# One transformer-like layer on one core: the products of a weight tile regrouped by width, and the tiles of the high weights moved by 192 bytes

## The chip, the core and the metric

The kernel runs on one core of a Trainium2 chip. The metric is the device time of one execution in microseconds. All weights lie in device memory in float32 and are streamed once per execution (277.83 MB read, by the page); everything else stays on the core.

## The reference, cut to what matters

One layer of a streaming encoder for 256 tokens of width 2048, with a memory of 256 more tokens:

```
u = rms_norm(h); proj = u @ w_in                       # 2048 -> 4944 columns
h = h + concat(gated_deltanet(...), mla_attention(...)) @ w_out
h = h + cross_attention(rms_norm(h), rms_norm(mem))    # xa_wq, xa_wk, xa_wv, xa_wo, all 2048 x 2048
u = causal_dwconv(rms_norm(h) @ w_up) + b              # 2048 -> 11264
h = h + (silu(gate) * up) @ w_down                     # 5632 -> 2048
return rms_norm(h)
```

Nearly all of the arithmetic is in the dense products with the seven weight matrices. All values are float32, and the result must be close to a float32 one.

## The kernel before, in words

**Three products for one.** Every float32 operand of a dense product is split into a high and a low part, both in the type that TensorE takes in one pass (float32r). The result is wh·xh + wh·xl + wl·xh. A tile of tokens holds xh in its columns 0 to 255 and xl in 256 to 511. So one step over 128 rows of the contraction, `kstep`, is two products: one of 512 columns with the high weights (wh on xh and xl at once, its halves are added after the sum), and one of 256 columns with the low weights (wl on xh). In this text they are H and L, and H and L of the same step are a pair. `kstep3` does the same in three products of 256 columns that add up in one place (wh on xh, wh on xl, wl on xh); the MLA part, the query projection, the cross-attention and the last block of the output use it. The value projection is written out by hand: the tokens of the memory are the weights there, and 512 columns of wh, wl and wh again are streamed over them (L981, L982, L983).

**Weight tiles.** `load_w` (L106) brings 128 x 1024 weights, eight steps, to a tile `raw` by a transfer on SyncE's queue. `split_w` makes wh by a rounding copy on ScalarE (L102) and wl by a subtraction on VectorE (L103). The three live in four buffers each of one pool. In the start, tiles come in halves (`piece`, L209).

**Order.** TensorE's order is the order of the code (a manual schedule, L189). The orders of the other engines are made by a scheduler from its own estimates. `kstep` alternates: H L, then L H, then H L, so that products of equal width follow each other in twos. In the DeltaNet and MLA parts the dense products serve as filler: a generator, `drawn` (L279), yields after each pair, and `fill(n)` and `until(n)` draw so many pairs between the small products, for instance 45 of them (`F_SOLVE`) while VectorE solves a small triangular system (tiles sol, prd, then tt).

**Places.** In the built program the tiles of tokens (u, om, od, mh, xq, xo, fx, ga, gb) begin at multiples of 256 bytes in each partition. So do kh, qh, pTx and vh, the operands of the cross-attention's small products. raw, wh and wl begin 64 bytes past such a multiple; a step within a weight tile is 512 bytes, so every 128 x 128 block of weights has the place of its tile.

Of the kernel before, what the change touches and what calls it, by code (L numbers as in the profile page):

```python
# [9 lines left out]
F32 = mybir.dt.float32  # L10
F32R = mybir.dt.float32r
# [6 lines left out]
F_BEFORE_MLA, F_BEFORE_DN1 = 8, 20  # L18
F_MLA, F_LEVEL, F_PRE, F_SOLVE = (6, 2, 4, 9), (3, 4, 5), (21, 6), 45
F_SCAN, F_NORM, F_SQ = 5, 28, 42  # L20

P = 128
T = 256
D = 2048
KC = D // P
DFF = 5632
NF = DFF // P
# [43 lines left out]
def trunk(ctx, tc, a):  # L71
    nc = tc.nc
    V, S, PE = nc.vector, nc.scalar, nc.tensor

    const = ctx.enter_context(tc.tile_pool(name="const", bufs=1))
    wpool = ctx.enter_context(tc.tile_pool(name="wpool", bufs=4))
# [5 lines left out]
    def psg():  # L82
        return pg.tile([P, 512], F32, name="psg", tag="psg")
# [12 lines left out]
    def split_w(raw, n, pieces=1):  # L96
        wh = wpool.tile([P, 1024], F32R, name="wh", tag="wh")
        wl = wpool.tile([P, 1024], F32R, name="wl", tag="wl")
        m = n // pieces
        for i in range(pieces):  # L100
            c = slice(i * m, (i + 1) * m)
            S.copy(wh[:, c], raw[:, c])  # L102
            V.tensor_sub(wl[:, c], raw[:, c], wh[:, c].bitcast(F32))  # L103
        return wh, wl

    def load_w(src, n=1024, pieces=1):  # L106
        raw = wpool.tile([P, 1024], F32, name="raw", tag="raw")
        nc.sync.dma_start(raw[:, 0:n], src)
        return split_w(raw, n, pieces)

    turn_ = [False]

    def kstep(ps, wh, wl, xh2, first, last):
        rev = turn_[0] and not first
        turn_[0] = not rev
        for lo in ((True, False) if rev else (False, True)):
            if lo:
                PE.matmul(ps[:, 0:256], wl, xh2[:, 0:256], start=False, stop=last, skip_group_check=True)  # L120
            else:
                PE.matmul(ps[:, 0:512], wh, xh2, start=first, stop=last, skip_group_check=True)  # L122

    def kstep3(ps, wh, wl, xh2, first, last):
        PE.matmul(ps[:, 0:T], wh, xh2[:, 0:T], start=first, stop=False)  # L125
        PE.matmul(ps[:, 0:T], wh, xh2[:, T:2 * T], start=False, stop=False)  # L126
        PE.matmul(ps[:, 0:T], wl, xh2[:, 0:T], start=False, stop=last)  # L127

    def gemm_block(w, nb, x, step=kstep):
        ps = psg()  # L130
        for hf in range(2):
            wh, wl = load_w(w[2 * nb + hf])
            for j in range(8):
                k = 8 * hf + j
                step(ps, wh[:, j * P:(j + 1) * P], wl[:, j * P:(j + 1) * P], x(k), k == 0, k == KC - 1)
        return ps
# [51 lines left out]
    u = hl_tile("u")  # L188
    ctx.enter_context(tc.manual_schedule(engines={mybir.EngineType.PE}))  # L189
    with ExitStack() as ph:  # L190
# [10 lines left out]
        first3 = []  # L201
        with tc.tile_pool(name="xpool", bufs=1) as xpl:
            xt = xpl.tile([P, KC, T], F32, name="xt")
            nc.sync.dma_start(sm[:, 0:KC], a["sm"][:, 0:KC])

            first3 += [psg(), psg(), psa("a")]
            w3 = {}

            def piece(nb, q):  # L209
                hf, c = q // 2, slice(q % 2 * 512, q % 2 * 512 + 512)  # L210
                if (nb, hf) not in w3:
                    w3[nb, hf] = [wpool.tile([P, 1024], t, name=nm, tag=nm)
                                  for nm, t in (("raw", F32), ("wh", F32R), ("wl", F32R))]
                raw, wh, wl = w3[nb, hf]
                nc.sync.dma_start(raw[:, c], a["w_in"][2 * nb + hf][:, c])
                S.copy(wh[:, c], raw[:, c])  # L216
                V.tensor_sub(wl[:, c], raw[:, c], wh[:, c].bitcast(F32))

            for q in range(4):
                for k in range(4 * q, 4 * q + 4, 2):  # L220
                    nc.sync.dma_start(xt[:, k:k + 2], a["x"][:, k:k + 2, :])
                    for i in (k, k + 1):
                        split_gain(u(i), xt[:, i], sm[:, C_MIX + i:C_MIX + i + 1])
                    if k % 4 == 0:
                        piece(0, q)
                for nb in range(3):
                    if nb:
                        piece(nb, q)
                    wh, wl = w3[nb, q // 2][1:]
                    for k in range(4 * q, 4 * q + 4):  # L230
                        j = k % 8
                        kstep(first3[nb], wh[:, j * P:(j + 1) * P], wl[:, j * P:(j + 1) * P], u(k), k == 0,
                              k == KC - 1)
            lead = load_w(a["w_in"][6], pieces=2)
            nc.sync.dma_start(cg, a["cg"])

            sqs = []
            for q in range(4):
                sqs.append(p1.tile([P, 4, T], F32, name="xsq", tag="qkv2", bufs=2))
                S.activation(sqs[q], xt[:, 4 * q:4 * q + 4], AF.Square)  # L240
                if q:
                    V.tensor_add(sqs[0], sqs[0], sqs[q])
            accs = [sqs[0][:, i] for i in range(4)]
            nc.sync.dma_start(sm[:, KC:NSM], a["sm"][:, KC:NSM])
            nc.sync.dma_start(co, a["co"][:, 0:NCO])
# [33 lines left out]
        def drawn():  # L279
            ready = {0: lead}  # L280
            ps = None
            i = 0
            while i < len(queue):
                for n in range(i, min(i + 1 + ahead[0], len(queue))):
                    if n not in ready:
                        ready[n] = load_w(queue[n][0], pieces=2)
                _, x, begin, first, last, done = queue[i]
                if begin:
                    begin()
                wh, wl = ready.pop(i)  # L290
                if first:
                    ps = psg()
                for j in range(8):
                    kstep(ps, wh[:, j * P:(j + 1) * P], wl[:, j * P:(j + 1) * P], x(j),
                          first and j == 0, last and j == 7)
                    if last and j == 7:
                        done(ps)
                    pos[0] += 1
                    for at_, f in [t for t in later if t[0] <= pos[0]]:
                        later.remove((at_, f))  # L300
                        f()
                    yield
                i += 1
# [77 lines left out]
        with ExitStack() as ms:  # L381
# [42 lines left out]
            ps = psa()  # L424
# [72 lines left out]
            ps = psa()  # L497
# [5 lines left out]
            ps = psa()  # L503
# [91 lines left out]
            for i in range(2):  # L595
                kn = mp.tile([P, 4, T], F32, name="kn", tag="kn")
                wh, wl = w_mla(i)
                for n in range(4):
                    ps = psg()
# [8 lines left out]
                wh, wl = w_mla(2 + i)  # L608
                for t in range(2):
                    ps = psg()  # L610
# [252 lines left out]
        od = hl_half("od")  # L863
# [72 lines left out]
    with ExitStack() as ph:  # L936
# [4 lines left out]
        for n in range(KC):  # L941
            wh, wl = load_w(a["w_out"][2 * n + 1])
            ps = psg()
            for j in range(8):
                kstep(ps, wh[:, j * P:(j + 1) * P], wl[:, j * P:(j + 1) * P], od[:, j], j == 0, j == 7)
            add_res(ps, n)
            if n < 8:
                mem_prep(8 + n)
# [10 lines left out]
        for n in range(KC):  # L959
            ps = gemm_block(a["xa_wk"], n, mh)  # L960
# [81 lines left out]

        def wo_half(ps, n, hf):
            wh, wl = load_w(a["xa_wo"][2 * n + hf])
            for j in range(8):
                k = 8 * hf + j
                kstep(ps, wh[:, j * P:(j + 1) * P], wl[:, j * P:(j + 1) * P], xo(k), k == 0, k == KC - 1)

        qhs, khs = {}, {}
        XS = float(512 ** -0.5)  # L1050
# [10 lines left out]
        xo = hl_tile("xo", x2pool)  # L1061
# [18 lines left out]
        for n in range(KC):  # L1080
            if n < 3:
                ps = pw[n]
            else:
                ps = psg()
# [10 lines left out]
    with ExitStack() as ph:  # L1095
# [3 lines left out]
        gk = lambda k: ga(k) if k < KC else gb[:, k - KC]  # L1099
# [35 lines left out]
        for n in range(KC):  # L1135
            ps = psg()
            for c in range(6):
                nk = 8 if c < 5 else 4
                o = n * NF * P + c * 1024
                wh, wl = load_w(a["w_down"][n, :, c * 1024:c * 1024 + nk * P], nk * P)  # L1140
                for j in range(nk):
                    k = 8 * c + j
                    (kstep if n < KC - 1 else kstep3)(ps, wh[:, j * P:(j + 1) * P], wl[:, j * P:(j + 1) * P],
                                                      gk(k), k == 0, k == NF - 1)
            if n < KC - 1:
                add_res(ps, n)
                accum_sq(oacc, hT[:, n], n == 0)
            else:
                V.tensor_add(hT[:, n], hT[:, n], ps[:, 0:T])
                lsq = small.tile([P, T], F32, name="lsq", tag="sq")  # L1150
                S.activation(lsq, hT[:, n], AF.Square)
            nc.gpsimd.tensor_scalar(hT[:, n], hT[:, n], sm[:, C_FIN + n:C_FIN + n + 1], None, ALU.mult)
# [119 lines left out]
```

## Time and profile before

| | us |
|---|---|
| median of 3 runs | 1577.72 (1575.12 to 1577.83) |
| the profiled execution | 1574.15 |
| its span, first to last instruction | 1572.3 |
| TensorE busy | 1542.3 (98%) |
| VectorE busy | 1117.3 (71%) |
| ScalarE busy | 888.5 (57%) |

The profile lists each engine's busy time and groups of equal instructions. A name such as psg<-fx,wh is output, streamed operand, weights. PE is TensorE; PEld is its weight loading, which overlaps the products. Matmuls overlap each other too: a product's listed length is longer than the distance at which products follow. So TensorE's share of 98% says that it hardly ever waits, and not how fast it works.

### The profile page before, as it was taken

How to read it: one execution, taken by the hardware profiler on the slowest of the kernel's cores; microseconds unless marked ns; L12 is line 12 of the kernel's file. 1: busy time of each engine (PE TensorE's matmuls, PEld its weight loads, DVE VectorE, ACT ScalarE, POOL GpSimd, SP SyncE). 2: the span in 40 equal slices, each digit the busy share in tenths (PEclk: the TensorE clock that was granted, in tenths of full speed). 3: DMA queues.
4: the chain of work that ended last, by engine and by line, in shares of the span. 5: the costliest groups of instructions: out<-in, count | busy, mean ns of one | idle time of the engine just before them, and what ended most of it. 6: DMA issues, size and time to landing. Idle time of an engine off the chain costs nothing.

```text
span 1572.3 us, 24569 instructions
## 1 busy us (share of the span) xinstructions
PE 1542.3 (98%) x9394; PEld 1357.5 (86%) x9394; DVE 1117.3 (71%) x1806; ACT 888.5 (57%) x1461; POOL 140.5 (9%) x145
## 2 busy tenths in 40 slices
PE   8999999999999999999999999999999999999996
PEld 7887887888888889999888888888888888888886
DVE  7887688697975555666777888888888886445453
ACT  7868666847664444454556666656665555434442
POOL 0232021002310000000110000000000000111112
PEclk9999999999999999999999999999999999999998
DMA  8564434354665555544555555555555556666663
GB/s 280 175 212 142 147 122 134 121 201 136 214 195 192 189 187 191 177 142 148 174 188 187 189 190 193 192 189 188 187 190 191 192 190 179 191 194 182 195 188 105
DMA packets 81494, 282.22 MB, mean 179 GB/s; under 512 B 9473, under 2 KB 9873, under 8 KB 81377
## 3 DMA queue, kind: packets, MB, share of 16 engines
q1 hardware_dynamic: 80064, 277.86, 54.7%
q0 software_dynamic: 1312, 2.80, 0.5%
q8 instruction: 73, 1.20, 0.3%
q14 instruction: 45, 0.36, 0.1%
HBM read 277.83 MB, written 2.11 MB: 178 GB/s over the span
## 4 chain that ended last, share of the span: by engine, by line
PE 88%; DVE 5%; ACT 4%; issue 1%; DMA 1%; POOL 0%; DVEq 0%; SPq 0%; ACTq 0%; POOLq 0%
PE psg L122 46%; PE psg L120 23%; PE psg L125 3%; PE psg L127 3%; PE psg L126 3%; DVE wl L103 2%; PE psg L983 2%; PE psg L982 2%; PE psg L981 2%; ACT wh L102 1%; DVE qkv L340 1%; PE psa L643 1%; PE psb L643 0%; PE psa L562 0%; DMA mt<-in_mem_dram 0%
## 5 line engine op out<-in xcount | busy, mean ns | idle before, releaser
L103 DVE TENSOR_TENSOR wl<-raw,wh 128x1024 fp32r<-128x1024 f32 (+1 forms) x602 | 641.0, 1071 | 278.5 <-ACT wh L102 271.3
L102 ACT CAST wh<-raw 128x1024 fp32r<-128x1024 f32 (+1 forms) x602 | 544.0, 915 | 393.7 <-PE psg L122 240.2
L122 PE MATMUL psg<-fx,wh 128*128 128x512 f32 x1408 | 439.8, 393 | 0.0
L120 PEld LDWEIGHTS psg<-fx,wl 128*128 128x128 f32 x1408 | 264.7, 188 | 59.8
L120 PE MATMUL psg<-fx,wl 128*128 128x256 f32 x1408 | 277.6, 279 | 0.0
L122 PEld LDWEIGHTS psg<-fx,wh 128*128 128x128 f32 x1408 | 212.2, 188 | 0.0
L122 PE MATMUL psg<-u,wh 128*128 128x512 f32 x608 | 200.6, 401 | 7.2 <-DVE u L149 7.2
L120 PEld LDWEIGHTS psg<-u,wl 128*128 128x128 f32 x608 | 115.3, 190 | 28.3 <-DVE wl L103 2.4
L140 ACT COPY half<-psg 128x256 f32<-128x256 f32 x142 | 52.6, 370 | 153.9 <-PE psg L122 153.7
L122 PE MATMUL psg<-gb,wh 128*128 128x512 f32 x420 | 133.4, 393 | 0.0
L120 PE MATMUL psg<-u,wl 128*128 128x256 f32 x608 | 130.3, 287 | 1.9 <-DVE wl L103 1.9
L122 PEld LDWEIGHTS psg<-u,wh 128*128 128x128 f32 x608 | 96.2, 190 | 9.5 <-ACT wh L216 7.2
L120 PEld LDWEIGHTS psg<-gb,wl 128*128 128x128 f32 x420 | 79.0, 188 | 17.9
L1112 DVE SCALAR_TENSOR_TENSOR y<-ub,sm,y 128x256 f32<-128x256 f32 x176 | 84.8, 482 | 3.5 <-ACT y L1110 0.3
L120 PE MATMUL psg<-gb,wl 128*128 128x256 f32 x420 | 82.8, 278 | 0.0
L122 PE MATMUL psg<-mh,wh 128*128 128x512 f32 x256 | 80.5, 394 | 0.0
L122 PE MATMUL psg<-xo,wh 128*128 128x512 f32 x256 | 80.4, 393 | 0.0
L141 DVE TENSOR_TENSOR ub<-psg,half 128x256 f32<-128x256 f32 x88 | 37.4, 425 | 59.7 <-ACT half L140 59.7
L122 PE MATMUL psg<-ga,wh 128*128 128x512 f32 x240 | 77.3, 393 | 0.0
L125 PE MATMUL psg<-xq,wh 128*128 128x256 f32 x256 | 71.2, 278 | 0.0
L126 PE MATMUL psg<-xq,wh 128*128 128x256 f32 x256 | 70.9, 277 | 0.0
L127 PE MATMUL psg<-xq,wl 128*128 128x256 f32 x256 | 70.9, 277 | 0.0
(411 smaller groups left out, 2430.1 us busy)
## 6 DMA issues: line engine op xcount, KB each, us to landing
raw<-in_w_up_dram SPq DMA_DIRECT2D x176, 512.0 KB, 3.5
raw<-in_w_down_dram SPq DMA_DIRECT2D x80, 512.0 KB, 4.3
raw<-in_w_in_dram SPq DMA_DIRECT2D x72, 512.0 KB, 3.9
raw<-in_w_out_dram SPq DMA_DIRECT2D x32, 512.0 KB, 3.6
raw<-in_xa_wk_dram SPq DMA_DIRECT2D x32, 512.0 KB, 3.5
raw<-in_xa_wv_dram SPq DMA_DIRECT2D x32, 512.0 KB, 3.4
raw<-in_xa_wq_dram SPq DMA_DIRECT2D x32, 512.0 KB, 3.5
raw<-in_xa_wo_dram SPq DMA_DIRECT2D x32, 512.0 KB, 3.4
```

What stands on the lines that cost most here:

```text
L102: S.copy(wh[:, c], raw[:, c])
L103: V.tensor_sub(wl[:, c], raw[:, c], wh[:, c].bitcast(F32))
L120: PE.matmul(ps[:, 0:256], wl, xh2[:, 0:256], start=False, stop=last, skip_group_check=True)
L122: PE.matmul(ps[:, 0:512], wh, xh2, start=first, stop=last, skip_group_check=True)
L125: PE.matmul(ps[:, 0:T], wh, xh2[:, 0:T], start=first, stop=False)
L126: PE.matmul(ps[:, 0:T], wh, xh2[:, T:2 * T], start=False, stop=False)
L127: PE.matmul(ps[:, 0:T], wl, xh2[:, 0:T], start=False, stop=last)
L140: S.copy(t, ps[:, T:2 * T])
L141: V.tensor_add(out, ps[:, 0:T], t)
L981: PE.matmul(pss[t], xh, wh[:, wk], start=(k == 0), stop=False)
L982: PE.matmul(pss[t], xh, wl[:, wk], start=False, stop=False)
L1112: V.scalar_tensor_tensor(y, b[:, j:j + T], sm[:, cw + j:cw + j + 1], y, ALU.mult, ALU.add)
```

## The change: groups by width, and another place for wh

`kstep` is replaced by a generator `ksteps` that takes the steps of a whole weight tile. It issues the products of 512 columns of all of them first, then those of 256 columns. It yields when 3, 6, 9, ... units are spent, an H being 2 units and an L 1: eight times in a tile of eight steps, so that `fill(n)` stands for the same number of columns as before. `kstep3` and the value projection keep their order. Two pads are taken in the weight pool: 192 bytes ahead of the buffers of wh, 64 ahead of those of wl. In the built program wh then begins at a multiple of 256 bytes, as the tokens do; wl and raw still lie 64 bytes past one.

```
+PADH, PADL = 192, 64
...
-    def kstep(ps, wh, wl, xh2, first, last):
-        rev = turn_[0] and not first
-        turn_[0] = not rev
-        for lo in ((True, False) if rev else (False, True)):
-            if lo:
-                PE.matmul(ps[:, 0:256], wl, xh2[:, 0:256], start=False, stop=last, skip_group_check=True)
-            else:
-                PE.matmul(ps[:, 0:512], wh, xh2, start=first, stop=last, skip_group_check=True)
+    def ksteps(ps, wh, wl, xs, first, last):
+        n = len(xs)
+        spent, due = 0, 3
+        for lo in (False, True):
+            m = T if lo else 2 * T
+            for j in range(n):
+                PE.matmul(ps[:, 0:m], (wl if lo else wh)[:, j * P:(j + 1) * P], xs[j][:, 0:m],
+                          start=first and not lo and j == 0, stop=last and j == n - 1, skip_group_check=True)
+                spent += 1 if lo else 2
+                if spent >= due:
+                    due += 3
+                    yield
...
-                    w3[nb, hf] = [wpool.tile([P, 1024], t, name=nm, tag=nm)
-                                  for nm, t in (("raw", F32), ("wh", F32R), ("wl", F32R))]
+                    tiles = []
+                    for nm, t, pad in (("raw", F32, 0), ("wh", F32R, PADH), ("wl", F32R, PADL)):
+                        if pad and not w3:
+                            wpool.tile([P, pad // 4], F32, name="pad" + nm, tag="pad" + nm, bufs=1)
+                        tiles.append(wpool.tile([P, 1024], t, name=nm, tag=nm))
+                    w3[nb, hf] = tiles
...
-                for j in range(8):
-                    kstep(ps, wh[:, j * P:(j + 1) * P], wl[:, j * P:(j + 1) * P], x(j),
-                          first and j == 0, last and j == 7)
+                for j, _ in enumerate(ksteps(ps, wh, wl, [x(j) for j in range(8)], first, last)):
```

All other calls of `kstep` become `run(ksteps(...))`, which draws the generator to its end: in the blocks of `gemm_block`, the output projections, and the down-projection but for its last block.

On TensorE, the first block of the gated up-projection (two weight tiles; fx are the tokens, psg the sum) stands in the order before as:

```order
L122 MATMUL psg_8555<-fx0_8463,wh_8558 128x512
L120 MATMUL psg_8555<-fx0_8463,wl_8559 128x256 x2
L122 MATMUL psg_8555<-fx0_8463,wh_8558 128x512 x2
L120 MATMUL psg_8555<-fx0_8463,wl_8559 128x256 x2
...
L122 MATMUL psg_8555<-fx0_8463,wh_8558 128x512
L122 MATMUL psg_8555<-fx1_8464,wh_8580 128x512
L120 MATMUL psg_8555<-fx1_8464,wl_8581 128x256 x2
```

and now, with L123 for both kinds of product:

```order
L123 MATMUL psg_8557<-fx0_8465,wh_8560 128x512 x8
L123 MATMUL psg_8557<-fx0_8465,wl_8561 128x256 x8
L123 MATMUL psg_8557<-fx1_8466,wh_8582 128x512 x8
L123 MATMUL psg_8557<-fx1_8466,wl_8583 128x256 x8
L185 MATMUL psc_8602<-cg_73,facc_8467 128x1 x2
L123 MATMUL psg_8608<-fx0_8465,wh_8611 128x512 x8
```

The sixteen runs of one or two products of a tile became two runs of eight; nothing else stands between them.

On TensorE in the first DeltaNet group, where it goes from filler to the first transposes of tt (L752 before, L765 now; u are the tokens), the order before is:

```order
L122 MATMUL psg_2706<-u0_77,wh_2643 128x512
L122 MATMUL psg_2706<-u1_78,wh_2668 128x512
L120 MATMUL psg_2706<-u1_78,wl_2669 128x256
L363 MATMUL psc_2733<-nsq_2581,cg_73 128x512
L120 MATMUL psg_2706<-u1_78,wl_2669 128x256
L122 MATMUL psg_2706<-u1_78,wh_2668 128x512
L752 MATMUL psa_2738<-cg_73,tt_2390 128x128 x4
L752 MATMUL psb_2745<-cg_73,tt_2435 128x128 x4
L122 MATMUL psg_2706<-u1_78,wh_2668 128x512
L120 MATMUL psg_2706<-u1_78,wl_2669 128x256 x2
```

and now:

```order
L123 MATMUL psg_2708<-u0_77,wh_2645 128x512 x8
L123 MATMUL psg_2708<-u0_77,wl_2646 128x256 x8
L123 MATMUL psg_2708<-u1_78,wh_2670 128x512 x2
L376 MATMUL psc_2735<-nsq_2583,cg_73 128x512
L123 MATMUL psg_2708<-u1_78,wh_2670 128x512
L765 MATMUL psa_2739<-cg_73,tt_2390 128x128 x4
L765 MATMUL psb_2746<-cg_73,tt_2436 128x128 x4
L123 MATMUL psg_2708<-u1_78,wh_2670 128x512 x5
```

The transposes now stand behind three H of a tile where they stood behind two pairs; the rest of the tile's H and all its L come after them.

VectorE's order, made by the scheduler, changes in small ways: between the first sol and tt it has 22 subtractions for half a weight tile where it had 21. On SyncE's queue the four loads of hT stand one weight load later.

## Rows read from the trace of the kernel before

**Rows 1.** Page: busy us (share) xcount; granted clock in 40 slices, tenths.

```profile
PE 1542.3 (98%) x9394; PEld 1357.5 (86%) x9394; DVE 1117.3 (71%) x1806; ACT 888.5 (57%) x1461; POOL 140.5 (9%) x145
...
PEclk9999999999999999999999999999999999999998
```

**Rows 2.** TensorE's waits, whole run: total us, times, longest.

```profile
PE psg L122 <- DVE u L149: 7.2, 1, 7.2
PE psa L752 <- DVE tt L722: 3.4, 1, 3.4
PE psb L581 <- ACT pT L578: 2.6, 2, 2.0
PE psg L120 <- DVE wl L103: 1.9, 1, 1.9
```

**Rows 3.** Windows, whole run, lines L122, L120, L125: PE, PEld busy (xcount).

```profile
0.00:1573.00 1573.00, 1093.19 (x3460) 526.55 (x3460) 1.00 0.56 179
...
0.00:1573.00 1573.00, 694.75 (x3460) 651.55 (x3460) 1.00 0.56 179
...
0.00:1573.00 1573.00, 120.31 (x428) 80.79 (x428) 1.00 0.56 179
```

**Rows 4.** Windows: start, up-projection, values; clock, DMA share, GB/s last.

```profile
core 0: us, PE busy (x) PEld busy (x) DVE busy (x) ACT busy (x) POOL busy (x), PEclk, DMA share, GB/s
8.49:11.05 2.56, 2.56 (x10) 2.17 (x9) 2.56 (x6) 2.56 (x7) 0.00 (x0) 1.00 1.04 391
...
560.42:576.90 16.48, 16.48 (x73) 13.52 (x72) 7.40 (x7) 6.32 (x6) 0.00 (x0) 1.00 0.57 182
836.55:1300.00 463.45, 463.45 (x2676) 406.59 (x2675) 378.76 (x589) 281.47 (x423) 0.00 (x0) 1.00 0.58 190
```

**Rows 5.** Lines, 836.55:1300: xcount | busy us, mean ns | idle.

```profile
L122 PE MATMUL psg<-fx,wh 128*128 128x512 f32 x1337 | 417.2, 393 | 0.0
L120 PE MATMUL psg<-fx,wl 128*128 128x256 f32 x1336 | 263.4, 279 | 0.0
```

**Rows 6.** Lines, value projection, 560.42:576.90.

```profile
L983 PE MATMUL psg<-wh,mh 128*128 128x512 f32 x25 | 9.8, 394 | 0.0
L982 PE MATMUL psg<-wl,mh 128*128 128x512 f32 x24 | 9.4, 392 | 0.0
L981 PE MATMUL psg<-wh,mh 128*128 128x512 f32 x24 | 9.3, 388 | 0.0
```

**Rows 7.** Timeline of PE at the start: start us, us, operation.

```profile
8.49 1.05 PE L122 MATMUL psg<-u,wh 128*128 128x512 f32 x2
...
9.77 1.05 PE L122 MATMUL psg<-u,wh 128*128 128x512 f32 x2
...
11.05 0.60 PE L122 MATMUL psg<-u,wh 128*128 128x512 f32 x1
```

**Rows 8.** Lines, kstep3 of a query block, 605.48:621.80.

```profile
L127 PE MATMUL psg<-xq,wl 128*128 128x256 f32 x49 | 13.5, 276 | 0.0
L126 PE MATMUL psg<-xq,wh 128*128 128x256 f32 x49 | 13.5, 276 | 0.0
```

**Rows 9.** Lines, kstep3 of the last output block, 1542.46:1557.65.

```profile
L125 PE MATMUL psg<-gb,wh 128*128 128x256 f32 x27 | 7.6, 281 | 0.0
```

**Rows 10.** Lines, kstep3 of the cross-attention's mix, 697.64:700.16.

```profile
L125 PE MATMUL psa<-pTx,vh 128*128 128x256 f32 x4 | 1.1, 283 | 0.0
```

**Rows 11.** Lines, whole run, query projection.

```profile
L125 PE MATMUL psg<-xq,wh 128*128 128x256 f32 x256 | 71.2, 278 | 0.0
L126 PE MATMUL psg<-xq,wh 128*128 128x256 f32 x256 | 70.9, 277 | 0.0
```

**Rows 12.** Timeline of PE around the DeltaNet solve.

```profile
254.24 1.12 PE L752 MATMUL psa<-cg,tt 128*128 128x128 f32 x4 [3.43 <-DVE tt L722]
```

**Rows 13.** Line L103 on DVE, 240:253: ns min/median/max.

```profile
L103 DVE TENSOR_TENSOR wl<-raw,wh x9: 681/683/685, 240.1 to 252.9; 128x512 fp32r<-128x512 f32 x9
```

More of the change, by code (lines that the diff above doesn't have):

```diff
@@ L109, in load_w, with run @@
         return split_w(raw, n, pieces)
-    turn_ = [False]
-    def kstep(ps, wh, wl, xh2, first, last):
-        rev = turn_[0] and not first
-        turn_[0] = not rev
-        for lo in ((True, False) if rev else (False, True)):
-            if lo:
-                PE.matmul(ps[:, 0:256], wl, xh2[:, 0:256], start=False, stop=last, skip_group_check=True)
-            else:
-                PE.matmul(ps[:, 0:512], wh, xh2, start=first, stop=last, skip_group_check=True)
+    def ksteps(ps, wh, wl, xs, first, last):
[10 more added lines that the diff above has]
+                    yield
+    def run(steps):
+        for _ in steps:
+            pass
     def kstep3(ps, wh, wl, xh2, first, last):
@@ L127, in kstep3, with gemm_block @@
         PE.matmul(ps[:, 0:T], wl, xh2[:, 0:T], start=False, stop=last)
-    def gemm_block(w, nb, x, step=kstep):
+    def gemm_block(w, nb, x, step=None):
         ps = psg()
@@ L132, in gemm_block @@
             wh, wl = load_w(w[2 * nb + hf])
+            if step is None:
+                run(ksteps(ps, wh, wl, [x(8 * hf + j) for j in range(8)], hf == 0, hf == 1))
+                continue
             for j in range(8):
@@ L229, in trunk @@
                     wh, wl = w3[nb, q // 2][1:]
[L230 to L233, printed above, removed]
+                    c = slice(q % 2 * 512, q % 2 * 512 + 512)
+                    run(ksteps(first3[nb], wh[:, c], wl[:, c], [u(4 * q + j) for j in range(4)], q == 0, q == 3))
             lead = load_w(a["w_in"][6], pieces=2)
@@ L943, in trunk @@
             ps = psg()
-            for j in range(8):
-                kstep(ps, wh[:, j * P:(j + 1) * P], wl[:, j * P:(j + 1) * P], od[:, j], j == 0, j == 7)
+            run(ksteps(ps, wh, wl, [od[:, j] for j in range(8)], True, True))
             add_res(ps, n)
@@ L1044, in wo_half @@
             wh, wl = load_w(a["xa_wo"][2 * n + hf])
-            for j in range(8):
-                k = 8 * hf + j
-                kstep(ps, wh[:, j * P:(j + 1) * P], wl[:, j * P:(j + 1) * P], xo(k), k == 0, k == KC - 1)
+            run(ksteps(ps, wh, wl, [xo(8 * hf + j) for j in range(8)], hf == 0, hf == 1))
         qhs, khs = {}, {}
@@ L1140, in trunk @@
                 wh, wl = load_w(a["w_down"][n, :, c * 1024:c * 1024 + nk * P], nk * P)
+                if n < KC - 1:
+                    run(ksteps(ps, wh, wl, [gk(8 * c + j) for j in range(nk)], c == 0, c == 5))
+                    continue
                 for j in range(nk):
                     k = 8 * c + j
-                    (kstep if n < KC - 1 else kstep3)(ps, wh[:, j * P:(j + 1) * P], wl[:, j * P:(j + 1) * P],
-                                                      gk(k), k == 0, k == NF - 1)
+                    kstep3(ps, wh[:, j * P:(j + 1) * P], wl[:, j * P:(j + 1) * P], gk(k), k == 0, k == NF - 1)
             if n < KC - 1:
```

## The prediction

> **What bounds the kernel now.** I read the page's busy times first: TensorE (PE) is busy 1542.3 of 1572.3 us and its clock is granted in full [rows 1]. Then its waits: only four are over 1 us, together 15.1 us, of which 7.2 are the start [rows 2]. So the time is the sum of the intervals at which products follow each other, and only those can be changed. The unit is a pair: one product of 512 columns (H, high weights) and one of 256 (L, low weights). There are 3460 of each [rows 3]. In the gated up-projection 463.45 us hold 1336.5 pairs [rows 4], 346.8 ns each.
>
> The listed length of a product is longer than its interval, since products overlap. H lists 393 ns and L 279 [rows 5]; 672 less 346.8 leaves 325.2, so 162.6 ns of each is tail. From here on I subtract 162.6 from a listed mean to get an interval: H 230.4, L 116.4. The chain of value products checks it: 394 + 392 + 388 [rows 6] gives 686.2 ns per three, and its 16.48 us hold about 72 products [rows 4], 686.7.
>
> What would be free of loss? At the very start the order HLLH takes 1.28 us per two pairs [rows 7], 640 ns a pair: 768 columns at one column per cycle of the 1.2 GHz level. (The clock column shows 1.00 there too [rows 4]; the pace is what I go by.) At 2.4 GHz that is 320.0: 213.3 for H, 106.7 for L. A pair of today thus loses 26.8 ns, 93 us over the kernel. More than that, fewer losses cannot give.
>
> And the loss is not a constant. Three chains of nothing but 256-column products, none waiting for anything, list 276, 281 and 283 ns, on all three of kstep3's lines [rows 8 to 10]: intervals of 113.4, 118.4 and 120.4. The first two run the same code (kstep3) with the same position of weights against tokens (64 bytes past a multiple of 256, tokens on one); the third has weights and tokens both on multiples of 256.
>
> The Trainium skill speaks against all of this. "SBUF — State Buffer", section "SBUF: two separate sides", says that TensorE never waits on anyone at the SBUF, and "TensorE: Matmul & The Clock Gate", section "Step-by-step: what each phase is for", that loading the next weights does not take read bandwidth from the running product. By these rules neither order nor position could matter and the change would be worth 0. The trace disagrees as far as 113.4 against 118.4 and 120.4 for equal products goes; that the position is the cause, no run here shows yet.
>
> **The change part by part.** *The order.* Each weight tile now runs as 8 H, then 8 L (in the start 4 and 4). No product is added or removed, nor any weight load.
>
> *L after L.* wl stays 64 bytes past a multiple of 256 and the tokens on one, as in the chains of rows 8 and 9. Bounds: 106.7 below, 120.4 above. I take 113.4: in rows 8 that rhythm, once reached, is kept for the whole stretch.
>
> *H after H, with wh now on a multiple of 256.* No row shows it. Below: 213.3. Above: 240.8, twice the 120.4 of the only chain in which both lie alike [rows 10]. The nearest rows are the three 512-column products of the value projection, 225.4, 229.4 and 231.4 [rows 6], where weights and streamed operand also differ by 64 bytes. I take 225.4, the best interval that this width shows.
>
> Pair: 225.4 + 113.4 = 338.8, which is 8.0 ns less than 346.8; x 3460 = -27.7 us.
>
> *Changes of width.* Each of the 432.5 tiles (3460 / 8) has two, H to L and L to H. If each fell into the slow rhythm of its width, 6.0 ns (231.4 - 225.4) and 5.0 (118.4 - 113.4): 4.8 us; if none did, 0. I take +2.4.
>
> *kstep3* keeps its order, but two of its three products use wh, moved too. There are 428 of each line [rows 3]; the query projection lists 278 for the first and 277 for the other two [rows 11], intervals 115.4, 114.4, 114.4. If the two went to 120.4: 428 x 11.0 = +4.7 us; the lower bound is that all go to 113.4, 428 x 4 = -1.7. I take +2.4.
>
> *Value projection.* 256 of its 384 products stream wh. Against their mean of 228.7: 213.3 gives -3.9 us, 240.8 gives +3.1. I take 0.
>
> *Covers and waits.* wl is first needed some 1.8 us later in a tile, so the 1.9 us wait for it [rows 2] may go: 0 to -1.9, I take -1. Nothing loses cover in return: in the up-projection VectorE works 378.76 of 463.45 us [rows 4], 283 ns a pair, and SyncE's loads use 0.58 of the DMA engines, so both stay hidden down to a pair of 283 ns. The start needs four token tiles before the first L instead of two; bounds 0 and 1.28 us, two pairs' time there [rows 7], I take +0.5. In the DeltaNet part TensorE waits 3.43 us for VectorE's tt [rows 12] behind 45 pairs of filling; these get 45 x 8.0 = 0.4 us shorter, and VectorE's order has 22 subtractions of half a weight tile between sol and tt where it had 21, 0.68 us each [rows 13]. Queued behind the waiting transposes is only the rest of the filler. +1.0, bounds 0 and +3. SyncE's four loads of hT stand one weight load later; several tiles are prefetched, so 0.
>
> Sum: -27.7 + 2.4 + 2.4 - 1 + 0.5 + 1 = -22.4 us. The profiled execution took 1574.15 us, its span 1572.3; the median of the runs shown is 3.57 above it. The sum is a difference, so I take it off the median: 1577.7 - 22.4 = 1555.3, say 1555.
>
> **The rivals.** *A: the loss is per weight load, not per column.* Then H loses what L loses, 6.7 ns, and runs at 220.0; the pair is 333.4, -13.4 x 3460 = -46.4, with the other +5.3 a time of 1537. For it: H has twice the columns behind which the same load hides. Against it: all H seen lose 12 ns or more. If wh's new place removed all loss of H (213.3), it would be 1513.
>
> The Trainium skill would put it lower still: "TensorE: Matmul & The Clock Gate", section "Back-to-back issue gap", gives N / 2.4 + 2.5 ns for a warm product, 215.8 and 109.2; as an estimate from that page a pair is 325, 75 us less than now. The trace does not agree for these operands: today's H is 14.6 ns above it.
>
> *B: the loss stays what it is.* 26.8 ns a pair are 13.4 per weight load, and 113.4 / 118.4 show that a chain can sit in a slow rhythm: with H at 230.4 and L at 116.4 nothing changes, and the changes of width and kstep3 cost nothing either: 1578. By the Trainium skill's rules quoted above ("SBUF — State Buffer") it would come out so too.
>
> *C: slower, since lying alike is the dearest place.* Rows 10 are the only chain in which weights and tokens share their place over 256 bytes, and it is the slowest of three, 7.0 ns above the best. Priced on H: 231.4 + 7.0 = 238.4; with L at 113.4 the pair is 351.8, +5.0 x 3460 = +17.3; kstep3 at its worst +4.7, changes of width +4.8: 1604. It decides from the point where H + L passes 346.8, so with L at 113.4 from an H of 233.4 on. Against it: those products are of 256 columns, where a load of 128 weight columns has to fit into one product; an H lasts twice as long.
>
> That the change does not do what it says I leave out: the order shows the groups, and the built program has wh on multiples of 256.
>
> **How the numbers follow.** Forecast (1543 to 1568, which is H at 222 to 229): 0.44. A: 0.20. B: 0.17. C: 0.19. The likeliest gives 1555. Within 0.2% (3.2 us), about what a measurement of this kernel can tell from no change: most of B, 0.12; faster 0.44 + 0.20 + 0.05 of B = 0.69; slower C, 0.19. For 8 in 10 the range leaves out the lower part of A (0.08) and the upper half of C (0.10): 1522 to 1592.
>
> **What would show it.** In the window of the up-projection the listed mean of the 512-column product falls from 393 to about 388 and that of the 256-column one from 279 to 276; 383 for the first is rival A, 393 and 279 unchanged are B, 396 or more for the first is C. The value projection and kstep3 tell the position alone, for their order is unchanged: kstep3's wh lines at 283 would say that lying alike costs. The waits of TensorE should stay under 20 us. I am wrong if the sum H + L does not fall, or if it falls while the time doesn't, which would mean a wait that I don't see: VectorE's wl at the turn from H to L.

## The result, and the profile after

| | before | after |
|---|---|---|
| median, us | 1577.71 (4 runs, 1575.12 to 1577.83) | 1585.68 (4 runs, 1583.86 to 1587.58) |
| the profiled execution, us | 1574.15 | 1586.30 |
| its span, us | 1572.3 | 1584.3 |

The ratio after/before is 1.0055, 95% interval 1.0042 to 1.0069. The change costs about 8 us where 22 us of gain were forecast. 1585.7 lies inside the range, but on the other side of zero. The two profiled executions differ by 12.0 us in span, mainly since before's is 3.6 us under its median; the pieces below are pieces of these 12.0.

The page of the changed kernel answers to [rows 1]: TensorE is as full as it was, and its clock is granted as before: at 1.00 but for 3.4 us at 0.50 in the DeltaNet solve and for the last stretch of the run, in both kernels. (The prediction read it as granted in full; that is not quite so.) So again it is the intervals that count, and a few waits.

```profile
PE 1550.3 (98%) x9394; PEld 1365.5 (86%) x9394; DVE 1111.3 (70%) x1806; ACT 877.9 (55%) x1463; POOL 141.1 (9%) x145
...
PEclk9999999999999999999999999999999999999998
```

TensorE's waits, whole run, answer to [rows 2]. Line numbers are higher by 13, and L123 is now both kinds of product.

```profile
PE psg L123 <- DVE u L162: 7.2, 1, 7.2
PE psa L765 <- DVE tt L735: 4.7, 1, 4.7
PE psb L594 <- ACT pT L591: 3.0, 4, 1.4
PE psa L512 <- DVE ex L508: 1.6, 1, 1.6
PE psa L718 <- DVE at L710: 1.6, 1, 1.6
PE psa L656 <- ACT xx L767: 1.0, 1, 1.0
```

The wait for wl (1.9) is gone, as forecast. But the wait for tt went from 3.4 to 4.7, and three that were not in the list before have come (ex, at, xx). All waits of 0.2 us and more add up to 22.4 us; before, 18.3. That is +4.1.

Now the pairs. One row of the windows view for the same stretch of the up-projection, the first line from before and the second from after:

```profile
850.00:1310.00 460.00, 460.00 (x2656) 403.54 (x2656) 375.09 (x583) 277.55 (x416) 0.00 (x0) 1.00 0.58 190
```

```profile
850.00:1310.00 460.00, 460.00 (x2649) 404.74 (x2648) 370.64 (x582) 264.24 (x416) 0.00 (x0) 1.00 0.58 189
```

460 us hold 1328 pairs before and 1324.5 after: 346.4 and 347.3 ns (the window of [rows 4], a little wider, gave 346.8 with three other products in it). The pair has not become shorter by 8.0 ns; it is 0.9 longer, times 3460 = +3.2 us. How this splits shows in the listed means of that window, which answer to [rows 5] (393 and 279):

```profile
L123 PE MATMUL psg<-fx,wh 128*128 128x512 f32 x1325 | 331.3, 392 | 0.0
L123 PE MATMUL psg<-fx,wl 128*128 128x256 f32 x1324 | 183.1, 281 | 0.0
```

H is 1 ns shorter and L 2 ns longer. With groups of eight the timeline itself can be read to 10 ns (start us, us, operation):

```profile
901.83 2.00 PE L123 MATMUL psg<-fx,wh 128*128 128x512 f32 x8
903.66 1.11 PE L123 MATMUL psg<-fx,wl 128*128 128x256 f32 x8
904.61 2.00 PE L123 MATMUL psg<-fx,wh 128*128 128x512 f32 x8
906.44 1.11 PE L123 MATMUL psg<-fx,wl 128*128 128x256 f32 x8
```

Eight H take 903.66 - 901.83 = 1.83 us and eight L 0.95: 229 and 118 ns each, 2.78 us a tile. Below, "intervals" are differences between the starts of successive products in the trace. In this tile they are 231, 236, 228, 232, 231, 227, 227, 225 for H, and 117 to 119 for L. Before, the steady pattern is H 226 or 236 and L 118 or 113, 2773 ns for eight pairs.

The chains whose order is unchanged tell of the place alone. Lines of the whole run, kstep3 of the query projection, which answer to [rows 11] (278, 277), and the value projection:

```profile
L135 PE MATMUL psg<-xq,wh 128*128 128x256 f32 x256 | 72.2, 282 | 0.0
L137 PE MATMUL psg<-xq,wl 128*128 128x256 f32 x256 | 72.2, 282 | 0.0
L136 PE MATMUL psg<-xq,wh 128*128 128x256 f32 x256 | 71.9, 281 | 0.0
...
L993 PE MATMUL psg<-wh,mh 128*128 128x512 f32 x128 | 50.6, 395 | 0.0
L995 PE MATMUL psg<-wh,mh 128*128 128x512 f32 x128 | 50.5, 394 | 0.0
L994 PE MATMUL psg<-wl,mh 128*128 128x512 f32 x128 | 50.4, 394 | 0.0
```

In kstep3 also L137 is 5 ns longer (277 before), whose weights, wl, did not move: the loss is not confined to the products whose weights did. Summed from the intervals of the whole run, kstep3 costs +3.3 us and the value projection +1.2. With +3.2 for the pairs and +4.1 of waits that is 11.8 of the 12.0 us.

### The profile page after: what moved, and what is told of

Same layout as the page of the kernel before. It is cut to its first block, busy times and chain, and to the rows that moved or that the text cites. A ratio compares the mean times of both kernels' runs of the same rounds, so it can differ in the third digit from the quotient of the medians.

```text
span 1584.3 us, 24755 instructions
## 1 busy us (share of the span) xinstructions
PE 1550.3 (98%) x9394; PEld 1365.5 (86%) x9394; DVE 1111.3 (70%) x1806; ACT 877.9 (55%) x1463; POOL 141.1 (9%) x145
## 5 line engine op out<-in xcount | busy, mean ns | idle before, releaser
L123 PE MATMUL psg<-fx,wh 128*128 128x512 f32 x1408 | 352.4, 392 | 0.8 <-DVE fx L162 0.8
L123 PEld LDWEIGHTS psg<-fx,wh 128*128 128x128 f32 x1408 | 252.1, 188 | 46.5 <-DVE fx L162 1.2
L123 PEld LDWEIGHTS psg<-fx,wl 128*128 128x128 f32 x1408 | 191.2, 189 | 13.4
L123 PE MATMUL psg<-fx,wl 128*128 128x256 f32 x1408 | 194.6, 281 | 0.0
L123 PE MATMUL psg<-u,wh 128*128 128x512 f32 x608 | 165.1, 404 | 7.2 <-DVE u L162 7.2
L123 PEld LDWEIGHTS psg<-u,wh 128*128 128x128 f32 x608 | 108.1, 191 | 27.3 <-ACT wh L233 7.2
L123 PE MATMUL psg<-gb,wh 128*128 128x512 f32 x420 | 106.3, 392 | 0.0
L123 PEld LDWEIGHTS psg<-u,wl 128*128 128x128 f32 x608 | 83.7, 190 | 7.4 <-issue 1.5
L123 PE MATMUL psg<-u,wl 128*128 128x256 f32 x608 | 89.2, 285 | 0.0
L123 PEld LDWEIGHTS psg<-gb,wh 128*128 128x128 f32 x420 | 74.7, 188 | 13.0
L137 PE MATMUL psg<-xq,wl 128*128 128x256 f32 x256 | 72.2, 282 | 0.0
L123 PE MATMUL psg<-mh,wh 128*128 128x512 f32 x256 | 64.2, 392 | 0.0
L123 PE MATMUL psg<-xo,wh 128*128 128x512 f32 x256 | 64.1, 392 | 0.0
L123 PEld LDWEIGHTS psg<-gb,wl 128*128 128x128 f32 x420 | 58.0, 189 | 4.7
L123 PE MATMUL psg<-ga,wh 128*128 128x512 f32 x240 | 60.0, 392 | 0.0
L123 PE MATMUL psg<-gb,wl 128*128 128x256 f32 x420 | 59.3, 281 | 0.0
```

The lines of the kernel that those rows point to most:

```text
L123: PE.matmul(ps[:, 0:m], (wl if lo else wh)[:, j * P:(j + 1) * P], xs[j][:, 0:m], start=first and not lo and j == 0, stop=last and j == n - ...
```

## Experiments

Two theories stood at the beginning: the place of wh costs and the groups don't, or the groups cost and the place doesn't.

**The groups alone.** The changed kernel without its pads:

```
-PADH, PADL = 192, 64
+PADH, PADL = 0, 0
```

> The changed kernel without the two pads: the products stand in groups of eight H and eight L, wh and wl both lie 64 bytes past a multiple of 256, as before the change. Theory 'place' (the new place of wh costs, the groups gain): L after L returns to the fast interval of 113.4 ns, listed mean 276, H lists about 392, the pair is 343 ns or less, and the time is about 1566 us, faster than before. Theory 'order' (the groups cost, the place does nothing): as the changed kernel, H 392 and L 281 listed, a pair of 348, 1582 to 1587 us. In both the query projection (kstep3) returns to a listed 277 to 278 if the place decides there.

Measured: 1578.05 us, before 1576.01; ratio 1.0014 (1.0005 to 1.0023). The groups are worth nothing, and cost 2 us; neither theory's time came out. kstep3 and the values are back at their times before (to 1 us), so there the place decides. The tile in the timeline:

```profile
901.95 2.02 PE L123 MATMUL psg<-fx,wh 128*128 128x512 f32 x8
903.81 1.07 PE L123 MATMUL psg<-fx,wl 128*128 128x256 f32 x8
904.72 2.02 PE L123 MATMUL psg<-fx,wh 128*128 128x512 f32 x8
```

Eight H take 1.86 us and eight L 0.91, in sum 2.77: as before the change. L runs in its fast rhythm (113 to 114 ns, one of 118 per tile), as the prediction wanted; H pays it back: 231 and 236 in turn, and 226 once.

**The place alone.** The kernel before, with its alternating order, and the pads:

```
+PADH, PADL = 192, 64
...
+                    for nm, t, pad in (("raw", F32, 0), ("wh", F32R, PADH), ("wl", F32R, PADL)):
```

> The kernel before with the two pads alone: wh on a multiple of 256 bytes, as the tokens; wl 64 past one; products in the order H L L H. Theory 'place': the pair grows from 346.8 to 350 ns or more, kstep3 in the query projection lists 282, as in the changed kernel, the value projection 3 ns more a product; time 1588 to 1595 us. Theory 'order': the pair stays at 346.8, listed 393 and 279; only kstep3 and the value projection grow, by 256 x 3 x 3.4 ns = 2.6 us and 384 x 3.2 ns = 1.2 us; time about 1581 us.

Measured: 1588.37 us, ratio 1.0087 (1.0072 to 1.0101). The place alone costs 12 us, more than the whole change. In its window of the up-projection:

```profile
850.00:1310.00 460.00, 460.00 (x2630) 400.79 (x2630) 373.18 (x580) 276.47 (x415) 0.00 (x0) 1.00 0.57 188
```

460 / 1315 = 349.8 ns a pair, 3.4 more than before, times 3460 = +11.8 us (intervals 233, 235, 119, 113 in turn). kstep3 and the values lose about the same +3.3 and +1.2 as in the changed kernel. (The profiled executions are 17.7 us apart, the medians 12.4: in the one of this kernel the granted clock is at 0.50 for 10.2 us ahead of the end, in that of before for 3.4.) By the two ratios, the groups give back 5 us at the new place; at the old place they cost 2.

**What a place costs, by itself.** A kernel of nothing but chains on TensorE: 24 H, 32 L, or 16 pairs H L, L H, for eleven pairs of places (tokens, weights), each chain after 0 to 3 products of 32 columns.

```
PLACES = ((0, 0), (0, 32), (0, 64), (0, 96), (0, 128), (0, 160), (0, 192), (0, 224), (64, 64), (64, 0), (64, 128))
```

> Nothing of the reference is computed: TensorE runs chains of products alone, with all other engines idle, for eleven pairs of places of tokens and weights over 256 bytes (tokens on 0, weights on 0, 32, 64, 96, 128, 160, 192, 224; then tokens on 64, weights on 64, 0, 128; tiles wha to whk in this order). Each has 4 x 24 products of 512 columns, 4 x 32 of 256 and 2 x 16 pairs in the order H L L H, each chain begun after 0 to 3 short products. Theory 'place': the intervals differ by place; at weights 64 past the tokens L after L is 113.4 ns in most chains and H after H 229 or less; at 0 apart L is 118 to 120 and H 231 or more. Theory 'order': all places agree within 1 ns, H after H is 231 and L after L 118, and 16 pairs of H L L H take less than 16 x (231 + 118). If the distance decides and not the place itself, tokens 64 with weights 64 is as 0 with 0, and 64 with 128 as 0 with 64.

Measured, intervals in ns once a chain is steady (pairs: over the last eight), at a granted clock of 1.00:

| tokens, weights | H | L | pair H L, L H |
|---|---|---|---|
| 0, 0 | 226.8 to 228 | 120.0 | 348.2 |
| 0, 32 | 233.4 | 118.4 | 351.4 to 351.8 |
| 0, 64 (before) | 233.4 | 113.3, once 117.8 | 346.7 |
| 0, 96 | 234.4 | 117.3, once 118.5 | 351.7 |
| 0, 128 | 232 to 233 | 118.8 to 120 | 348.4 |
| 0, 160 | 233.5 | 119.9 | 350.0 and 353.2 |
| 0, 192 | 228.8 | 117.8, once 113.3 | 345.0 |
| 0, 224 | 233.3 | 116.7 to 117.8 | 346.6 |
| 64, 64 | 226.8 | 120.0 | 348.4 |
| 64, 0 | 228.8 | 117.8 | 345.0 |
| 64, 128 | 233.4 | 113.3 or 117.8 | 346.6 |

The last three rows equal those of the same difference with tokens at 0: the difference of the places (weights minus tokens) modulo 256 bytes decides, not either place. Lying alike is the best place for H and, with 160, the worst for L; the theory 'place' had H the wrong way round (231 or more at 0, 229 or less at 64). And for one and the same place L has two rhythms. Why the difference matters inside the chip, no run here shows. One chain of 32 L at (0, 0) in the timeline: 49.73 - 45.81 is 3.92 us, of which the first interval, behind a short product, is 0.20, and the other 31 are 120 ns each.

```profile
45.81 4.08 PE L55 MATMUL psl<-xs,wla 128*128 128x256 f32 x32
49.73 0.29 PE L42 MATMUL psm<-xs,wha 128*128 128x32 f32 x2
```

**Groups, by themselves.** The same, with groups of 8 H and 8 L (four times) and of 16 and 16 (three times), for sixteen pairs of places (wh, wl), tokens at 0:

```
HIGH, LOW = (64, 0, 192, 128), (64, 192, 224, 0)
```

> Nothing of the reference is computed: TensorE alone runs groups, for sixteen pairs of places (high weights 64, 0, 192, 128 bytes past the tokens over 256; within each, low weights 64, 192, 224, 0 past; tiles wha to whp in this order). Each pair runs 4 times 8 H and 8 L, then 3 times 16 H and 16 L. Theory 'distance' (what the distance over 256 bytes between weights and tokens is, sets the interval, whatever stood before): a tile of 8 H and 8 L takes 8 x (H + L) with H 233.4, 227, 228.8, 233 and L 113.4, 113.4, 116.7, 120 by place; so high 0 with low 64 gives 2723 ns, and the changed kernel's 2780 would come from its other engines. Theory 'entry' (which of two rhythms a group runs in is set by the phase in which it begins, and H at 0 needs some products to settle): high 0 with low 64 gives 2780 here too, high 64 with low 64 gives 2773, and groups of 16 at high 0 are cheaper per product than groups of 8 by 2 ns an H.

Measured per tile of eight pairs, steady: (64, 64) 2773 ns, (0, 64) 2780, (192, 64) 2747; the others from 2741 to 2813, above 2773 in most. The second is the changed kernel, (wle, whe), the third the best that repeats from tile to tile, (wli, whi):

```profile
130.62 2.00 PE L46 MATMUL psh<-xs,whe 128*128 128x512 f32 x8
132.46 1.11 PE L51 MATMUL psl<-xs,wle 128*128 128x256 f32 x8
133.40 2.00 PE L46 MATMUL psh<-xs,whe 128*128 128x512 f32 x8
...
245.39 2.00 PE L46 MATMUL psh<-xs,whi 128*128 128x512 f32 x8
247.22 1.07 PE L51 MATMUL psl<-xs,wli 128*128 128x256 f32 x8
248.13 2.00 PE L46 MATMUL psh<-xs,whi 128*128 128x512 f32 x8
```

1.84 and 0.94 us: the tile of the changed kernel, with no other engine at work and no DMA. So traffic of other engines is no part of this tile's length: 'distance' falls and 'entry' holds. With wh at 192, H takes 1.83 us, about as at 0, and L 0.91. In groups of 16 at (0, 64), H settles at 227 ns from its sixth product on and is 1.3 ns cheaper than in groups of 8 (2 were expected), L stays at 118. And (192, 64) is not safe: its third group of 16 runs at 233 ns an H and 118 an L, so H too can be slow at a place where it was 229.

**What chooses L's rhythm.** n H at three places of wh (n from 1 to 16), then 32 L, wl always at 64:

```
HIGH = (64, 0, 192)
COUNTS = (1, 2, 3, 4, 5, 6, 7, 8, 10, 12, 16)
```

> Nothing of the reference is computed, only chains on TensorE: n H (n from 1 to 16) with wh at 64, 0 or 192, then 32 L with wl always at 64; each twice. Theory: the rhythm of the L (113.3 or 117.8 ns) is chosen in the first two or three of a group by how the group was entered, and kept for all 32; so for one and the same place of wl both rhythms appear, depending on n and on the place of wh before, and within a group no change is seen. Rival 1: the place of wh before decides alone: after wh at 0 always 117.8, after 64 and 192 always 113.3, whatever n. Rival 2: the slow rhythm is a settling time: after 8 to 20 products every group reaches 113.3, so that the mean of the last 8 of 32 is 113.3 everywhere.

Measured: both rhythms from one place of wl, kept to the end of the 32; both rivals fall. With wh at 64 (the clock was low in the very first chain) an odd n gives 113.3 and an even n 117.8, without exception. Here n = 7, then n = 8:

```profile
72.21 1.87 PE L46 MATMUL psh<-xs,wha 128*128 128x512 f32 x7
73.92 3.80 PE L51 MATMUL psl<-xs,wla 128*128 128x256 f32 x32
77.56 0.18 PE L42 MATMUL psm<-xs,wha 128*128 128x32 f32 x1
...
82.96 2.11 PE L46 MATMUL psh<-xs,wha 128*128 128x512 f32 x8
84.90 3.93 PE L51 MATMUL psl<-xs,wla 128*128 128x256 f32 x32
88.67 0.18 PE L42 MATMUL psm<-xs,wha 128*128 128x32 f32 x1
```

The 32 L take 77.56 - 73.92 = 3.64 us after seven H, and 88.67 - 84.90 = 3.77 after eight. With wh at 0 they are fast after 2, 3, 4 and 6 H, and slow after 1 and after 7, 8, 10, 12 and 16, where H has settled at 225 to 227; after 5, one of each. With wh at 192 they are fast after 1, 5, 7, 8, 10 and 16, slow after 2, 4, 6 and 12; after 3, one of each. The theory said two or three products of a group choose; with wh at 0 and n = 5 or 6 it took three or four (118, 124, 118, then 113). The part that n plays holds for this kernel, where the H begin behind a short product. With both weights at 64 and eight H behind a group of L, the L that follow are fast, in the kernel of groups by themselves and in the run of the groups alone (0.91 us for eight). So the count alone does not choose; what stands ahead of the H counts too.

**Groups at the better place.** The changed kernel with wh at 192 and wl at 64:

```
-PADH, PADL = 192, 64
+PADH, PADL = 128, 128
```

> The changed kernel with wh 192 bytes past a multiple of 256 (pads of 128 and 128) and wl at 64 as before. In the chains of products alone, H at 192 took 228.8 ns from its first product on, and L at 64 either 113.4 or 117.8. Theory 'distance': listed means 391 to 392 for H and 276 for L, a pair of 342.2, 346.8 - 342.2 = 4.6 x 3460 = 16 us less than before, some 2 us given back in the value projection (its distance becomes 64: 233 for 229); about 1563 us. Theory 'entry': H 228.8, but L may sit in the slow rhythm as in the changed kernel, listed 281; then the pair is 346.6 and the time 1577 to 1580 us.

Measured: 1575.30 us, before 1576.19; ratio 0.9996 (0.9988 to 1.0005), no change. The pairs do gain: 460 us hold 1340 of them, 343.3 ns. Two groups in the timeline:

```profile
904.38 2.00 PE L123 MATMUL psg<-fx,wh 128*128 128x512 f32 x8
906.21 1.07 PE L123 MATMUL psg<-fx,wl 128*128 128x256 f32 x8
907.12 2.00 PE L123 MATMUL psg<-fx,wh 128*128 128x512 f32 x8
```

From 904.38 to 907.12 it is 2.74 us: 1.83 for eight H, 0.91 for eight L. Neither theory's time came out. What is given back: kstep3 +3.1, values +0.8, and waits of 22.5 us against 18.3; nor do the pairs gain everywhere (see the run of both together).

**Where the waits come from.** Groups everywhere but in the filler, where H L, L H returns; no pads:

```
 def drawn():
...
-                for j, _ in enumerate(ksteps(ps, wh, wl, [x(j) for j in range(8)], first, last)):
+                for j in range(8):
+                    kstep(ps, wh[:, j * P:(j + 1) * P], wl[:, j * P:(j + 1) * P], x(j),
+                          first and j == 0, last and j == 7)
```

> Groups by width everywhere except in the filler of the DeltaNet and MLA parts, where H L, L H stays; no pads, so wh and wl lie 64 bytes past as in the kernel before. With groups everywhere (e1) the first om product starts 3.6 us later than before and nothing after it loses. Theory: the groups cost nothing as such, but the small products of the DeltaNet part then stand behind other amounts of filler and wait longer (18.3 us of waits before, 21.1 in e1); with the filler as before, om starts at 334.0 us as before, and the ratio is 1.000 (0.999 to 1.001). Rival: groups cost by themselves, at every change of width; then the ratio stays at 1.0014 and the loss is spread over the stages in proportion to their pairs.

Measured: 1576.99 us, before 1576.23; ratio 1.0004 (0.9995 to 1.0012), and the first product on om at 334.0 us, as before (337.8 with groups everywhere). That is what the theory said. The times alone do not separate this kernel from the one with groups everywhere (1.0005 to 1.0023), so it rests on the waits and on om's start in one profiled execution each; of those 3.8 us about 0.7 is granted clock, at 0.50 for 6.8 us in the solve with groups everywhere and for 3.4 in this run and before. The waits in the stretch of the DeltaNet solves, 216 to 281 us, first of the changed kernel, then of this one:

```profile
PE psa L765 <- DVE tt L735: 4.7, 1, 4.7
PE psa L718 <- DVE at L710: 1.6, 1, 1.6
PE psb L792 <- DVE tt L778: 0.5, 1, 0.5
PE psa L792 <- DVE tt L778: 0.3, 1, 0.3
```

```profile
PE psa L778 <- DVE tt L748: 3.4, 1, 3.4
PE psb L805 <- DVE tt L791: 0.5, 1, 0.5
```

7.1 against 3.9 us; groups everywhere without the pads show the same four waits, 7.0. `fill(n)` draws as many columns as before, but in the filler of a tile the H now come first, and the scheduler gives VectorE another order; the wait for tt is longer by 1.3, and that for at is new. Which of these two makes the waits longer was not tried apart.

**Both together, as a faster version.** The same kernel with the pads 128 and 128.

> The same, but with pads of 128 and 128 bytes: wh lies 192 bytes past a multiple of 256, wl 64 as before. Theory: a tile of 8 + 8 in these places takes 2747 ns where before takes 2773 (m2 and e3), 26 ns less on some 367 tiles outside the filler, -9.5 us; kstep3 +3.1 and the value projection +0.8 as in e3; no more waits than before, where e3 had 4.8 us more. Sum -5.6 us: ratio 0.9964 (0.9950 to 0.9980). Rival: what e3 gave back was not the waits of the filler; then it stays at 0.9996.

Measured: 1573.32 us, before 1576.23; ratio 0.9984 (0.9975 to 0.9992). It is faster than the kernel before by some 2.5 us, half of what was expected. The up-projection gains as in the run with groups everywhere at this place (2681 products in 460 us, 343.2 ns a pair), and the waits are down at 17.6 us. But the down-projection gains little: between 1316 and 1540 us a pair takes 345.5 ns where it took 346.7, some 1.4 us less than expected on 646 pairs. There about every second tile of ga runs slow, here the first of two:

```profile
1330.96 2.03 PE L134 MATMUL psg<-ga,wh 128*128 128x512 f32 x8
1332.83 1.11 PE L134 MATMUL psg<-ga,wl 128*128 128x256 f32 x8
1333.78 2.01 PE L134 MATMUL psg<-ga,wh 128*128 128x512 f32 x8
```

Its eight H take 1.87 us and its eight L 0.95, the slow rhythm of both.

In the profiled execution, which is 2.6 us over the median, the first product on om starts at 338.9 instead of 334.0. H L, L H at (192, 64) takes 350.4 ns in the filler where it took 347.6. But most of the delay is the granted clock: it is at 0.50 for 3.4 us at 69 us and again at 209, and for 6.8 us from 256.8, where the kernel before has its only such stretch, of 3.4. First before, then this kernel:

```profile
69.00:72.00 3.00, 3.00 (x20) 2.61 (x19) 2.12 (x5) 2.99 (x6) 0.00 (x0) 1.00 0.81 221
...
250.00:265.00 15.00, 11.57 (x71) 10.00 (x70) 10.83 (x24) 9.43 (x15) 2.36 (x1) 0.89 0.33 106
```

```profile
69.00:72.00 3.00, 3.00 (x11) 2.52 (x10) 2.38 (x5) 2.97 (x6) 0.00 (x0) 0.51 0.70 182
...
209.00:212.00 3.00, 3.00 (x11) 2.52 (x11) 2.27 (x3) 0.52 (x2) 0.79 (x1) 0.50 0.02 5
...
250.00:265.00 15.00, 11.77 (x54) 9.23 (x53) 10.50 (x32) 8.15 (x14) 0.00 (x0) 0.77 0.43 141
```

A clock of 0.50 is the 1.2 GHz level: 11 products where 20 ran. By the starts of the same products in both kernels, the three stretches cost about 1.6, 1.5 and 1.4 us, 4.5 of the 4.9. The medians do not differ by the clock: its mean over all twelve executions is 0.9946, over those of before beside them 0.9943. Just ahead of the falls at 69 and 209 us TensorE had idled, 1.75 us for wl and 1.98 us for pT:

```profile
67.84 0.51 PE L124 MATMUL psg<-u,wl 128*128 128x256 f32 x2 [1.75 <-DVE wl L106]
...
208.19 0.70 PE L607 MATMUL psb<-pT,vm 128*128 128x256 f32 x2 [1.98 <-ACT pT L604]
```

The kernel before idles there as long, 1.94 us for wl and 2.0 for pT, and its clock stays at 1.00. Why the one falls and the other doesn't stays open.

**Both weights at 192.** As the last, with wl moved too (a third pad keeps the tokens where they are):

```
-PADH, PADL = 128, 128
+PADH, PADL = 128, 0
...
+                    if not w3:
+                        wpool.tile([P, 32], F32, name="padend", tag="padend", bufs=1)
```

> As e4 (groups outside the filler, H L L H in it), but wh and wl both lie 192 bytes past a multiple of 256; a third pad of 128 bytes keeps the tokens on one. In e4 the filler alone was 4.7 us longer than before (om starts at 338.7 us, 334.0 before), as in e2, where H L L H met unlike places of wh and wl. Theory: H L L H depends on both places; with both at 192 m1 has 345.0 to 347.1 ns per pair where both at 64 have 347.0, so om starts again at 333.5 to 334.5. Groups of 8 ran in 2772 and then 2741 ns per tile in these places (m2), so they give 0 to -11.7 us on some 367 tiles; kstep3 and value +3.9 as in e3. Sum: 1569 to 1580 where before is 1577, ratio 0.9985 as the middle. Rival: the cost of the filler in e4 was wh at 192 alone, whatever wl's place; then om starts at 338.7 again and the ratio is 1.001 or more.

Measured: 1576.79 us, before 1577.14; ratio 0.9994 (0.9985 to 1.0003). In the filler the pair is at 346.3 ns (347.6 before, 350.4 in the run above), as the theory had it, but om still starts at 338.5. The forecast of om's start did not come true in the profiled execution, and not for the rival's reason: the clock is at 0.50 in the same three stretches (3.4, 3.4 and 6.8 us), which by the starts of the same products cost about 4.5 us, the whole delay. The groups in the up-projection alternate here between tiles with fast and with slow L, 88 of each.

## Why the prediction was wrong, point by point

**What bounds the kernel** was right: before, the intervals of the pairs, not waits; of the 11.8 us lost, though, 4.1 are waits. The sign that the prediction itself named for being wrong came: H + L did not fall. That the place of the weights against the tokens bears on the intervals, which the prediction left open, is shown by the table of places (L 113.3 to 120.0, H 226.8 to 234.4 for equal products). As the prediction read the Trainium skill's "SBUF — State Buffer", section "SBUF: two separate sides", and "TensorE: Matmul & The Clock Gate", section "Step-by-step: what each phase is for", nothing could depend on the place; these chains disagree, and where in the chip the loss arises stays open.

**L after L at 113.4: the step that failed.** Measured 118, where the mean before was 116.4 [rows 5]. The prediction took from the kstep3 chains [rows 8] that this place of wl and tokens has the fast rhythm and that "that rhythm, once reached, is kept". The second half is right: the 32 L of the entry experiment keep theirs. The first is wrong: the same place has two rhythms, and the products ahead of the group choose. Behind eight H with wh at 0 it is the slow one, in 175 of the 176 tiles of the changed kernel's up-projection and every time in both kernels of chains that have it. 4.6 ns x 3460 = 16 us of the missing 31 on the pairs. The listed 281 of [rows 9], same code and places as 276 in [rows 8], was the sign that one place has two rhythms; the prediction used it for the changes of width and in rival B, but not for L after L itself.

**H after H, with wh moved, at 225.4: a term sized wrong.** Measured 229.7 over a tile. The value itself exists: H at 0 settles at 225 to 227, and its bounds (213.3 to 240.8) held. That it was met is luck: it was read off the value projection, where weights minus streamed operand is 192, for which the table has 228.8. And H at 0 needs five products to settle, at 228 to 236, where a tile has eight. 4.3 x 3460 = 15 us. Together: +3.2 us where the sum had -27.7.

**Changes of width, +2.4.** Wrong in kind: it was priced as an event at each change. A change of width costs a few ns itself (in the groups by themselves at (64, 64) the first L of a tile takes 118 or 119 and the rest 113); what counts is the rhythm in which the group behind it then stays.

**kstep3, +2.4**: +3.3, within its bounds, but all three lines went to 281 or 282, that of the unmoved wl as well, and none to the 283 of [rows 10]. **Value projection, 0**: +1.2, within bounds.

**Waits.** For wl -1.9 as bounded. At the start, the first 96 products end 0.4 us later (26.45 instead of 26.07), for +0.5. The DeltaNet part was put at +1 (0 to +3): it has +3.2 in the solves and +3.0 for pT, ex and xx, so that waits, put at 0 in all (-1 and +1), came out at +4.1 with the gain on wl and smaller changes taken in. Only the wait of [rows 12] had been looked at; the one for at, new and 1.6 us, stands at the same turn from filler to small products. The runs show the order in the filler as the cause: waits of 17.6 to 19.1 us in the three with the old order there, 21.2 to 22.5 in the three with groups there (18.3 before). Whether it acts through TensorE's order or VectorE's was not tried apart.

**The rivals.** A fell: no steady chain of H came under 226. The estimate by the Trainium skill's "TensorE: Matmul & The Clock Gate", section "Back-to-back issue gap" (215.8 and 109.2, by a formula that the section gives for an isolated product), was reached by no chain here either; the best steady ones are 226.8 and 113.3. B is nearest for the pairs, 347.3 against 346.4, though by accident: both parts moved and cancelled. C had the side right and the mechanism wrong. Its price was put on H; yet H is cheapest where both lie alike. It is L that is dearest there, 120.0, as [rows 10] said for products of that width, and L's weights had not been moved.

## What to carry to other kernels

Where products follow each other without waits, a listed mean is a mix of rhythms: look at the starts of successive products before taking the best one as the price of a new order. Price an order by the whole repeating unit, best by a kernel of that unit alone (here 2780 ns against 2773), for a mean of parts that were measured apart does not add up. And where filler is drawn in pieces, a new order inside it can move the waits around it, as it did here: change the dense stretches alone first.

## What the runs showed of the hardware

- For float32r products at a granted clock of 1.00 the distance of weights and streamed operand within 256 bytes of a partition bears on the interval, with nothing else at work: 226.8 to 234.4 ns for 512 columns, 113.3 to 120.0 for 256. Best for 512 columns is distance 0 (226.8); for 256 columns the same distance is, with 160, the worst (120.0).
- At distances of 64 and 192 a chain of 256-column products has two rhythms, 113.3 and 117.8 ns; the one in which it ran by its sixth product it held to the end of 32. The products ahead choose. At 192, 512 columns have run at 229 and at 233.
- Much of the spread between executions of one kernel goes with its granted clock. Over 70 runs of the kernel before, the span is on average 1576.7 us at a mean clock of 0.992, 1574.7 at 0.994 and 1572.0 at 0.996. Of two kernels that are 3 us apart, compare the clocks as well as the times.
